# Experts 1 to 7 in order of token count, loaded from addresses read at run time

## The chip, the cores and the metric

One core of a Trainium2 chip runs the whole program. The metric is the device time of one execution in microseconds (us); lower is better.

## The reference

The program is a decoder trunk of two layers on 256 tokens of width 1024, in float32. Each layer is a mixer (a convolution group and a gated group) and a feed-forward part. The first layer's feed-forward part is dense; the second's, which the change is about, routes every token to the best two of eight experts:

```python
def moe_swiglu(h, router, wg, wu, wd):
    ht = h.reshape(B * S, D)                       # 256 x 1024
    logits = jnp.einsum('td,de->te', ht, router)   # 256 x 8
    top_vals, top_idx = lax.top_k(logits, TOP_K)   # TOP_K = 2
    gates = jax.nn.softmax(top_vals, axis=-1)
    dense_gate = jnp.sum(jax.nn.one_hot(top_idx, 8) * gates[..., None], axis=1)
    out = jnp.zeros_like(ht)
    for e in range(8):                             # wg, wu: 1024 x 2816, wd: 2816 x 1024
        out = out + dense_gate[:, e:e + 1] * swiglu(ht, wg[e], wu[e], wd[e])
    return out

def swiglu(h, wg, wu, wd):
    return (silu(h @ wg) * (h @ wu)) @ wd
```

The 256 tokens make 512 token slots, 64 for an expert on average; how many each expert gets depends on the input.

## The kernel before

Mixer 0, the dense part and mixer 1 come first, and their instructions are ordered by a small planner in the kernel. The experts' stage, `moe`, is written out in program order.

**Weights.** The host lays all weights out as blocks of 128 x 2048 floats (1 MiB each) in the order in which they are used. An expert has 33 of them: 8 for hidden chunk 0, 8 for chunk 1, 6 for chunk 2, and 4, 4 and 3 for the rows of the down projection that belong to these chunks. A load (`load_raw`, line 306) is one DMA of one block from SyncE's queue. There is a ring of 19 buffers (`rawof`, tile name `wraw`); `upto` issues loads ahead as far as the ring goes, so SyncE waits until the load 19 places earlier has had its last use, and then issues. The addresses are constants. The first 19 expert loads are all of expert 0 and are issued during mixer 1, before the routing is known.

**Slots.** An expert's tokens get slots in groups of 32, and at most three groups (`NG = 3`, 96 slots). `one_hot` makes a 0/1 matrix of tokens by slots; `gather` multiplies it with the normalised tokens to get the slots' columns `xg`, for two experts at a time: experts 0 and 1 ahead of the stage, and the pairs after that in the middle of experts 1, 3 and 5.

**Products.** TensorE (PE) holds the slots of one group (32 columns, repeated on four column strips) and streams the weights past them (`side_by_side`, line 1249), so that a group costs the same whatever number of tokens it holds. `hidden` is one chunk of gate and up products (`pg`, `pu`, for chunk 2 also `pgu`), `turn` transposes the chunk (`ptr`), `down` multiplies it by its rows of the down projection (`mpd`), `back` (`ppt`) turns the one-hot matrix, and `combine` (`pcomb`) puts the results back in token order and adds them to the residual `xs` with the gate as a factor. On PE an expert's order is: chunk 0, the last part of the down projection of the expert before and its combine, chunk 1, down 0, chunk 2, `back`, (gather), down 1.

**The third group.** It runs only if the expert has more than 64 tokens. For every one of the six stages of an expert (`hidden` three times, `down` three times) `arms` does groups 0 and 1 and then branches on the count, which PE has read into a register:

```python
def arms(c, body, blank):
    body(range(NG - 1))
    with tc.If(c > (NG - 1) * GW) as full:
        body((NG - 1,))
    with full.Else():
        blank()
```

`blank` (line 1255) is a product with zeros that opens and closes the third group's PSUM region. The branch itself stands at line 1235. Transposes, `back` and `combine` do three groups for every expert.

**More than 96 tokens.** At the end all engines read the largest count and skip a further pass (`further`) when it fits 96 slots.

Of the kernel before, what the change touches and what calls it, by code (L numbers as in the profile page):

```python
# [33 lines left out]

NG = 3
# [133 lines left out]
def weight_plan():  # L169
# [48 lines left out]
    def expert_loads(key, w, e, c0, n, k0, k1):  # L218
        per = 2048 // n
        plan[key, e] = plan.get((key, e), [])  # L220
        for k in range(k0, k1, per):
            plan[key, e].append(len(loads))
            loads.append([(w, (0, e), k, k + per, c0, n)])

    def rows(e, b):
        expert_loads(f"d{b}", "moe_wd", e, 0, D, 8 * b, min(8 * b + 8, KF))

    for e in range(E):
        for b in range(3):
            for c0, n in (WIDE[b:b + 1] if b < 2 else WIDE[b:]):  # L230
                for w in ("moe_wg", "moe_wu"):
                    expert_loads(f"h{b}", w, e, c0, n, 0, KD)
            if b or e:
                rows(e - (b == 0), (b - 1) % 3)
    rows(E - 1, 2)
    return loads, units, plan, rest


def weight_blocks(inputs):

    import numpy as np
    loads = weight_plan()[0]
# [12 lines left out]
def hybrid_trunk(  # L255
# [28 lines left out]
    st = dict(next=0, load=0, split=0, ahead=0)  # L284
# [14 lines left out]
    def load_raw(i, h=None):  # L299
        n = sum((k1 - k0) * w for _, _, k0, k1, _, w in loads[i])  # L300
# [93 lines left out]
    def upto(i):  # L394

        for j in range(st["ahead"], min(i + 1, len(loads))):
# [33 lines left out]
    G.memset(tri8, 1.0)  # L430
    G.affine_select(out=tri8, in_=tri8, compare_op=OP.is_gt, fill=0.0, base=0,
                    pattern=[[1, E], [-1, E]], channel_multiplier=0)
# [83 lines left out]
    def mixer(l, sg, nxt, rt=None):  # L516
        with ExitStack() as c2:
# [514 lines left out]
            def e_slots(t):  # L1032
# [14 lines left out]
                small(lambda: rt.one_hot(rt.oh, 0, t), (("pos", t),), (("oh", t),), 0.335)  # L1047
                if t:
                    small(lambda: V.tensor_copy(rt.icnt, pp[:, 2 * E:3 * E]), (nm,), ("icnt",), 0.075)
# [111 lines left out]
    class Route:  # L1161


        def __init__(self, pool, top):
# [11 lines left out]
            self.icnt = pool.tile([P, E], I32, name="icnt")  # L1176
# [8 lines left out]
        def one_hot(self, oh, e0, t):  # L1185
            V.tensor_tensor(oh[:, t], iot[:, None, :SL].to_broadcast([P, 2, SL]),
                            self.pos[:, t, e0:e0 + 2, None].to_broadcast([P, 2, SL]), op=OP.is_equal)

    def moe(sg, rt):
        with ExitStack() as c2:  # L1190
            gup = c2.enter_context(tc.tile_pool(name="gu", bufs=4, space=PSUM))
            pdp = c2.enter_context(tc.tile_pool(name="pd", bufs=2, space=PSUM))
            r, xn, pos, gate = sg.r, rt.xn, rt.pos, rt.gate
            st["late"] = c2.enter_context(tc.tile_pool(name="late", bufs=LATE_RAW, side="right"))
            pool = c2.enter_context(tc.tile_pool(name="experts", bufs=1))
            zero = pool.tile([P, 512], BF16, name="zero")
            G.memset(zero, 0.0)
# [6 lines left out]
            def next_pair(e0):  # L1204
                rt.oh = rt.one_hot_tile()
                for t in range(NT):
                    rt.one_hot(rt.oh, e0, t)

            def gather(e0):

                xg = rt.pool.tile([P, KD, 2 * SL], F32, name="xg", tag="big0") if e0 // 2 % 2 else pool.tile([P, KD, 2 * SL], F32, name="xg")
                oh = rt.oh

                def part(k2, ps, eng):
                    for q in range(2):
                        k = k2 * 2 + q
                        for t in range(NT):
                            T.matmul(ps[:, q * 2 * SL:(q + 1) * 2 * SL], xn[:, t, k * P:(k + 1) * P],
                                     oh[:, t].rearrange("p e s -> p (e s)"), start=(t == 0), stop=(t == NT - 1))
                    copy(eng, xg[:, k2 * 2:k2 * 2 + 2].rearrange("p k s -> p (k s)"), ps[:, :4 * SL])  # L1220
# [7 lines left out]

            def arms(c, body, blank):

                body(range(NG - 1))
                if c is None:
                    body((NG - 1,))
                    return
                with tc.If(c > (NG - 1) * GW) as full:
                    body((NG - 1,))
                with full.Else():
                    blank()
# [13 lines left out]
            def blank(banks, w):  # L1252

                b, o = divmod((NG - 1) * w, 512)
                T.matmul(banks[b][:, o:o + w], zero[:, :P], zero[:, :w], start=(o == 0), stop=True, skip_group_check=True)  # L1255

            def hidden(e, b, xg, c):
# [4 lines left out]
                o = e % 2 * SL  # L1262
                w = 256 if b < 2 else 128
                nb = -(-NG * w // 512)
# [7 lines left out]
                def body(gs):  # L1272
                    def x_(k):
                        return lambda g, q: xg[:, k, o + g * GW:o + (g + 1) * GW]
                    nl = 4 * w // 256
                    for j in range(2):
                        for k in range(KD):
                            side_by_side(banks[j], w, gs, x_(k), k == 0, k == KD - 1, [cols(nl * j, k, 4 * w, q * w, w) for q in range(4)])
                    if both:
                        for k in range(KD):  # L1280
                            side_by_side(both, P, gs, x_(k), k == 0, k == KD - 1, [cols(2 * nl + q // 2, k, 256, q % 2 * P, P) for q in range(4)])

                def blanks():
                    for v in banks:
                        blank(v, w)
# [286 lines left out]
```

## Time and profile before

| what | value |
|---|---|
| median of 3 runs | 1195.4 us (1195.16 to 1205.32) |
| the profiled execution: its own time | 1198.35 us |
| the profiled execution: its span, first to last instruction | 1196.6 us |
| experts' stage, first product of expert 0 to the last down part of expert 7 | 399.69 to 1172.40 us |
| what stands behind that (last down part, combine, final norm, output) | 24.2 us |
| mean granted TensorE clock | 0.961 |

The profile's time lies 1.75 us over its span. Busy times are those of one engine; TensorE's products are pipelined and their ends are modelled, so that "busy" is not "at its peak", and a product's start is the surer number.

### The profile page before, as it was taken

Reading aid. Unit: us, or ns where it says so; the run is one execution under the profiler, and the core shown is the slowest. Engines: PE = TensorE matmul, PEld = TensorE weight load, DVE = VectorE, ACT = ScalarE, POOL = GpSimd, SP = SyncE. Lnnn points to the kernel's source line nnn. Section 1 sums busy time; section 2 is a strip of 40 time slices with the busy share of each in tenths; the row PEclk is TensorE's granted clock in tenths of the full one; section 3 lists DMA queues with packets and bytes.
Section 4 is the critical chain, followed back from the end, with each engine's and each line's share of the span. In section 5 each row is a group of like instructions: output and inputs, shape, how many; then the busy total and the mean of one; then the engine's idle time right before and its main releaser. Section 6 shows DMA issues by size and latency. Waiting matters only on the chain. (4 is left out here: it accounts for less than half of the span.)

```text
span 1196.6 us, 33425 instructions
## 1 busy us (share of the span) xinstructions
PE 1072.5 (90%) x15484; PEld 791.6 (66%) x15484; DVE 319.6 (27%) x641; ACT 277.5 (23%) x474; POOL 143.9 (12%) x115
## 2 busy tenths in 40 slices
PE   8999999999999986986998997799799889989884
PEld 7767888887978645555656655556656666677562
DVE  5985555545895100010010010010001000100102
ACT  6665444444684000000000000100000010000002
POOL 3872000000895000000000000000000000000001
PEclk9999999999999887998999998999999999999998
DMA  8934455454843599999699789978969966888951
GB/s 308 392 133 150 176 178 183 176 202 141 304 147 121 223 420 369 369 377 366 280 401 409 314 342 369 374 299 349 407 243 382 378 272 236 368 360 349 391 206 39
DMA packets 52002, 344.06 MB, mean 288 GB/s; under 512 B 6596, under 2 KB 8444, under 8 KB 11388
## 3 DMA queue, kind: packets, MB, share of 16 engines
q1 hardware_dynamic: 48876, 339.40, 71.4%
q8 instruction: 143, 2.34, 0.8%
q10 hardware_dynamic: 2960, 2.13, 0.6%
q14 instruction: 23, 0.19, 0.0%
HBM read 340.46 MB, written 1.05 MB: 285 GB/s over the span
## 5 line engine op out<-in xcount | busy, mean ns | idle before, releaser
L1249 PE MATMUL mpd<-wraw,ah 128*32 128x256 f32 x3520 | 208.1, 393 | 8.3 <-issue 7.9
L1249 PE MATMUL pu<-wraw,xg 128*32 128x256 f32 (+1 forms) x3840 | 189.2, 351 | 19.4 <-issue 19.4
L1249 PE MATMUL pg<-wraw,xg 128*32 128x256 f32 (+1 forms) x3840 | 183.8, 345 | 12.4 <-DVE xs L1370 6.7
L1249 PEld LDWEIGHTS mpd<-wraw,ah 128*32 128x32 f32 x3520 | 124.3, 114 | 86.0 <-issue 22.3
L1249 PEld LDWEIGHTS pu<-wraw,xg 128*32 128x32 f32 x3840 | 124.7, 113 | 76.9 <-issue 22.3
L1249 PEld LDWEIGHTS pg<-wraw,xg 128*32 128x32 f32 x3840 | 118.2, 110 | 71.9 <-issue 10.8
L315 ACT ACTIVATE whi<-wraw 128x1024 fp32r<-128x1024 f32 x110 | 116.4, 1059 | 117.0 <-PE pd L376 31.1
L1293 DVE TENSOR_TENSOR sg<-sg,pu 128x512 f32<-128x512 f32 (+2 forms) x40 | 21.7, 554 | 447.0 <-ACT sg L1292 236.8
L1292 ACT ACTIVATE sg<-pg 128x512 f32<-128x512 f32 (+2 forms) x40 | 19.6, 490 | 473.5 <-PE pg L1255 143.8
L320 DVE TENSOR_TENSOR wlo<-wraw,whi 128x1024 fp32r<-128x1024 f32 x73 | 89.3, 1224 | 84.1 <-ACT whi L315 82.5
L1435 POOL TENSOR_TENSOR wraw<-xs,wraw 128x512 f32<-128x512 f32 (+1 forms) x4 | 3.9, 1002 | 793.1 <-DVE xs L1370 793.1
L320 POOL TENSOR_TENSOR wlo<-wraw,whi 128x1024 fp32r<-128x1024 f32 x37 | 89.2, 2430 | 14.4 <-ACT whi L315 13.5
L824 DVE SCALAR_TENSOR_TENSOR acc<-big,cwt,acc 128x256 f32<-128x256 f32 x199 | 86.8, 481 | 1.7
L1227 ACT ACTIVATE ah<-ptr 128x512 f32<-128x512 f32 (+1 forms) x24 | 13.5, 561 | 179.6 <-PE ptr L1307 179.6
L1249 PE MATMUL pgu<-wraw,xg 128*32 128x128 f32 x1280 | 44.0, 288 | 12.4 <-issue 12.4
L1249 PEld LDWEIGHTS pgu<-wraw,xg 128*32 128x32 f32 x1280 | 39.8, 117 | 14.6 <-issue 14.5
L757 PE MATMUL mm<-xh,whi 128*128 128x256 f32 x128 | 37.7, 294 | 2.0 <-ACT whi L315 2.0
L759 PE MATMUL mm<-xh,wlo 128*128 128x256 f32 x128 | 36.5, 285 | 0.5 <-DVE wlo L320 0.5
L343 PE MATMUL pu<-whi,xh 128*128 128x512 f32 (+1 forms) x96 | 36.5, 381 | 0.0
L758 PE MATMUL mm<-xl,whi 128*128 128x256 f32 x128 | 36.5, 285 | 0.0
L343 PE MATMUL pg<-whi,xh 128*128 128x512 f32 (+1 forms) x96 | 36.2, 377 | 0.0
L344 PE MATMUL pg<-wlo,xh 128*128 128x512 f32 (+1 forms) x96 | 36.1, 376 | 0.0
(226 smaller groups left out, 1253.1 us busy)
## 6 DMA issues: line engine op xcount, KB each, us to landing
wraw<-in_blocks_dram SPq DMA_DIRECT2D x316, 1024.0 KB, 11.7
wraw<-in_blocks_dram SPq DMA_DIRECT2D x10, 512.0 KB, 10.4
xs<-in_x_dram SPq DMA_DIRECT2D x2, 512.0 KB, 7.5
wst<-in_sgu_w_dram ACTq DMA_DIRECT2D x2, 256.0 KB, 15.4
grow<-in_norm_ffn_dram ACTq DMA_DIRECT2D x2, 256.0 KB, 3.2
wraw<-in_norm_final_dram SPq DMA_DIRECT2D x1, 512.0 KB
out_dram<-wraw SPq DMA_DIRECT2D x4, 128.0 KB, 2.2
out_dram<-wraw SPq DMA_DIRECT2D x2, 256.0 KB
```

The lines of the kernel that those rows point to most:

```text
L315: A.activation(ready[i][0][:, :w], src, AF.Copy)
L320: eng.tensor_sub(ready[i][1][:, :w], src, ready[i][0][:, :w].bitcast(F32))
L343: T.matmul(bank, xs_[0][:, c, sl], w, start=first, stop=False)
L344: T.matmul(bank, xs_[0][:, c, sl], lo, start=False, stop=False)
L757: T.matmul(o, hi[:, ws], xt[0][:, k], start=(k == 0), stop=False)
L758: T.matmul(o, hi[:, ws], xt[1][:, k], start=False, stop=False)
L759: T.matmul(o, lo[:, ws], xt[0][:, k], start=False, stop=(k == KD - 1))
L824: V.scalar_tensor_tensor(accp, src, wv, accp if w else pa, op0=OP.mult, op1=OP.add)
L1227: A.activation(o, i, AF.Copy)
L1249: T.matmul(region(banks, w, g, q), x_(g, q), srcs[q], start=first and g % (512 // w) == 0, stop=last, skip_group_check=True)
L1292: A.activation(h[:, i, :n], banks[0][i][:, :n], AF.Silu)
L1293: V.tensor_tensor(h[:, i, :n], h[:, i, :n], banks[1][i][:, :n], op=OP.mult)
```

## The change

Expert 0 stays first and is loaded from constant addresses. The other seven go in order of their token count, largest first. `places`, on VectorE, ranks the counts, writes the first block of each place's expert into an integer tile, and moves positions and counts from expert order to place order; the gates follow among the operations that are done beside expert 0. SyncE reads one integer for each place (`value_load`) and adds the block's number to it, so that the loads of places 1 to 7 have register addresses. The host lays out the blocks expert by expert, with the same blocks in the same order inside an expert.

The number of groups is fixed by place, `GROUPS = (3, 3, 3, 3, 3, 2, 2, 2)`, and there is no branch in the main pass: `arms`, `blank`, the zero tile and PE's reading of the counts are gone, and each stage goes over all its groups inside its loop over weight rows. Transposes, `back` and `combine` do only the groups of the place. Gathers are for place 0 alone (ahead of the stage), then for pairs 1-2, 3-4, 5-6 (in the middle of places 0, 2 and 4) and for place 7 alone (in place 6). The further pass runs if a place's count is over its slots.

```diff
+GROUPS = (3, 3, 3, 3, 3, 2, 2, 2)
 ...
     def load_raw(i, h=None):
+        if i < rest["load"]:
+            src = lambda cs: blocks[i, :, cs]
+        else:
+            e, j = loads[i]
+            if e == 0:
+                src = lambda cs: blocks[rest["load"] + j, :, cs]
+            else:
+                if e not in st["at"]:
+                    st["at"][e] = nc.sync.value_load(st["place"][0:1, e:e + 1], ...)
+                src = lambda cs: blocks[bass.ds(st["at"][e] + j, 1), :, cs].rearrange("o p c -> (o p) c")
 ...
-                nc.sync.dma_start(rawof[i][:, cs], blocks[i, :, cs])
+                nc.sync.dma_start(rawof[i][:, cs], src(cs))
 ...
+        def sorting(self, pool):
 ...
+            for e in range(E):
+                G.memset(self.cap[:, e:e + 1], float(GROUPS[e] * GW))
+                G.memset(self.e8[:, e:e + 1], float(e))
+                G.memset(self.base[:, e:e + 1], float(rest["load"] + e * LOADS))
+            earlier(self.tri)
 ...
+        def pick(self, o, v):
+            V.tensor_tensor(self.sort[0], self.order, v[:, None, :].to_broadcast([P, E, E]), op=OP.mult)
+            V.tensor_reduce(o, self.sort[0], axis=AX.X, op=OP.add)
+
+        def places(self):
+            c, (gt, eq) = self.crank, self.sort
+            V.tensor_copy(c, self.cnt)
+            V.tensor_scalar(c[:, 0:1], c[:, 0:1], 1024.0, None, op0=OP.add)
+            other, mine = c[:, None, :].to_broadcast([P, E, E]), c[:, :, None].to_broadcast([P, E, E])
+            V.tensor_tensor(eq, other, mine, op=OP.is_equal)
+            V.tensor_tensor(gt, other, mine, op=OP.is_gt)
+            V.tensor_tensor(eq, eq, self.tri, op=OP.mult)
+            V.tensor_tensor(gt, gt, eq, op=OP.add)
+            V.tensor_reduce(self.first, gt, axis=AX.X, op=OP.add)
+            V.tensor_tensor(self.order, self.first[:, None, :].to_broadcast([P, E, E]),
+                            self.e8[:, :, None].to_broadcast([P, E, E]), op=OP.is_equal)
+            self.pick(self.first, self.base)
+            V.tensor_copy(self.place, self.first)
+            for t in range(NT):
+                self.pick(self.ppos[:, t], self.pos[:, t])
+            self.pick(self.pcnt, self.cnt)
 ...
-            def arms(c, body, blank):
-            def blank(banks, w):
-            def hidden(e, b, xg, c):
+            def hidden(e, b, xg, ng):
 ...
+                for j in range(2):
+                    for k in range(KD):
+                        side_by_side(banks[j], w, range(ng), x_(k), k == 0, k == KD - 1, ...)
 ...
             xg, steps = gather(0, 1)
             for j, f in enumerate(steps):
                 f(lambda: gu_tile("pgat"), V if j % 2 else A)
+            rt.places()
 ...
             def largest():
+                V.tensor_sub(rt.pcnt, rt.pcnt, rt.cap)
 ...
+            def by_place(t):
+                rt.pick(rt.pgate[:, t], gate[:, t])
 ...
-            experts(xg, lambda e: nc.tensor.value_load(rt.icnt[0:1, e:e + 1], min_val=0, max_val=S), ...)
+            experts(xg, GROUPS, lambda e: later if e == 0 else ())
 ...
-            with tc.If(cnt > SL):
+            with tc.If(cnt > 0):
```

## Rows read from the trace of the kernel before

**Rows 1.** The page: engines' busy time, and the costliest group of products.

```profile
PE 1072.5 (90%) x15484; PEld 791.6 (66%) x15484; DVE 319.6 (27%) x641; ACT 277.5 (23%) x474; POOL 143.9 (12%) x115
...
L1249 PE MATMUL mpd<-wraw,ah 128*32 128x256 f32 x3520 | 208.1, 393 | 8.3 <-issue 7.9
```

**Rows 2.** Busy time by window, experts 0 to 7: length, engines, clock, DMA.

```profile
399.69:481.64 81.95, 66.47 (x1227) 45.39 (x1227) 6.25 (x24) 5.37 (x12) 0.00 (x0) 0.88 0.86 349
481.64:578.39 96.75, 77.92 (x1403) 54.25 (x1402) 8.52 (x20) 8.34 (x18) 0.00 (x0) 0.93 0.92 374
578.39:680.87 102.48, 95.08 (x1939) 63.81 (x1938) 7.28 (x16) 6.15 (x13) 0.00 (x0) 0.97 0.84 340
680.87:776.07 95.20, 80.74 (x1452) 54.05 (x1451) 8.52 (x20) 8.34 (x18) 0.00 (x0) 0.93 0.90 364
776.07:877.48 101.41, 91.55 (x1940) 61.80 (x1939) 7.27 (x16) 6.15 (x13) 0.00 (x0) 1.00 0.85 346
877.48:989.79 112.31, 102.52 (x2019) 70.94 (x2018) 8.61 (x20) 8.33 (x18) 0.00 (x0) 0.97 0.81 325
989.79:1089.34 99.55, 93.67 (x1987) 66.95 (x1986) 7.27 (x16) 6.14 (x13) 0.00 (x0) 1.00 0.82 331
1089.34:1172.40 83.06, 73.12 (x1420) 48.11 (x1419) 7.53 (x17) 6.60 (x15) 0.00 (x0) 0.96 0.70 278
```

**Rows 3.** Waits of PE's products from 480 us: sum, times, longest.

```profile
PE pg L1255 <- issue: 19.0, 5, 5.6
```

**Rows 4.** Waits of SyncE's queue, whole span: sum, times, longest.

```profile
SPq L306 <- PE pg L1249: 149.0, 11, 19.7
```

**Rows 5.** Two windows in which loads are queued; last columns: DMA share, GB/s.

```profile
1104.00:1124.00 20.00, 18.65 (x334) 11.60 (x326) 4.60 (x12) 1.25 (x3) 0.00 (x0) 1.00 0.99 395
1054.00:1068.00 14.00, 11.18 (x367) 10.21 (x359) 0.42 (x1) 0.60 (x1) 0.00 (x0) 1.00 1.02 420
```

**Rows 6.** PE's timeline in expert 3, two groups: zero products and the gather.

```profile
725.13 0.37 PE L1255 MATMUL pg<-zero 128*128 128x256 bf16 x1 [3.43 <-issue]
...
725.65 9.63 PE L1249 MATMUL mpd<-wraw,ah 128*32 128x256 f32 x128
...
758.26 0.29 PE L1255 MATMUL pg<-zero 128*128 128x128 bf16 x1 [5.08 <-issue]
...
758.69 2.79 PE L1348 MATMUL ppt<-ident,oh 128*32 128x128 f32 x48
...
764.82 7.11 PE L1249 MATMUL mpd<-wraw,ah 128*32 128x256 f32 x128
772.11 0.85 PE L1307 MATMUL ptr<-ident,sg 128*128 128x128 f32 x6 [0.18 <-PEq L1235]
```

**Rows 7.** PE's timeline in expert 6, three groups: start, length, what, idle before.

```profile
1003.63 3.64 PE L1249 MATMUL pg<-wraw,xg 128*32 128x256 f32 x64
...
1010.54 7.95 PE L1249 MATMUL mpd<-wraw,ah 128*32 128x256 f32 x144
...
1019.23 2.87 PE L1365 MATMUL pcomb<-eo,pt 32*128 32x256 f32 x48
1023.05 7.11 PE L1249 MATMUL pg<-wraw,xg 128*32 128x256 f32 x128 [0.95 <-DVE xs L1370]
...
1063.43 0.97 PE L1249 MATMUL pu<-wraw,xg 128*32 128x128 f32 x28 [1.95 <-issue]
...
1069.65 0.97 PE L1249 MATMUL pgu<-wraw,xg 128*32 128x128 f32 x28 [2.53 <-issue]
1070.44 0.27 PE L1249 MATMUL pg<-wraw,xg 128*32 128x128 f32 x1
...
1075.88 1.07 PE L1348 MATMUL ppt<-ident,oh 128*32 128x128 f32 x29
```

**Rows 8.** The window of the gather ahead of the stage.

```profile
392.44:399.69 7.25, 7.25 (x32) 7.03 (x32) 0.68 (x2) 0.98 (x2) 0.00 (x0) 0.74 0.93 391
```

**Rows 9.** VectorE's operations of the routing, by shape: busy, mean ns.

```profile
L1025 DVE TENSOR_TENSOR dg<-lg 128x64 f32<-128x64 f32 x2 | 1.5, 746 | 0.1
```

More of the change, by code (lines that the diff above doesn't have):

```diff
@@ L216, in weight_plan, with expert_loads, expert_blocks @@
     rest = dict(load=len(loads))
[L218 to L226, printed above, removed]
+    def expert_loads(key, e):
+        first = {"h0": 0, "h1": 8, "h2": 16, "d0": 22, "d1": 26, "d2": 30, "end": 33}
+        last = list(first.values())[list(first).index(key) + 1]
+        plan[key, e] = list(range(len(loads), len(loads) + last - first[key]))
+        loads.extend((e, j) for j in range(first[key], last))
     for e in range(E):
         for b in range(3):
-            for c0, n in (WIDE[b:b + 1] if b < 2 else WIDE[b:]):
-                for w in ("moe_wg", "moe_wu"):
-                    expert_loads(f"h{b}", w, e, c0, n, 0, KD)
+            expert_loads(f"h{b}", e)
             if b or e:
-                rows(e - (b == 0), (b - 1) % 3)
-    rows(E - 1, 2)
+                expert_loads(f"d{(b - 1) % 3}", e - (b == 0))
+    expert_loads("d2", E - 1)
     return loads, units, plan, rest
+LOADS = 33
+def expert_blocks(e):
+    out = []
+    for w, i0, i1 in (("h", 0, 1), ("h", 1, 2), ("h", 2, 4), ("d", 0, KF)):
+        if w == "d":
+            out += [("moe_wd", (0, e), k, k + 2, 0, D) for k in range(0, KF, 2)]
+        else:
+            out += [(m, (0, e), k, k + 2048 // n, c0, n) for c0, n in WIDE[i0:i1] for m in ("moe_wg", "moe_wu") for k in range(0, KD, 2048 // n)]
+    assert len(out) == LOADS
+    return [[v] for v in out]
 def weight_blocks(inputs):
     import numpy as np
-    loads = weight_plan()[0]
+    loads, _, _, rest = weight_plan()
+    loads = loads[:rest["load"]] + [v for e in range(E) for v in expert_blocks(e)]
     out = np.zeros((len(loads), P, 2048), np.float32)
@@ L282, in hybrid_trunk @@
     loads, units, plan, rest = weight_plan()
-    st = dict(next=0, load=0, split=0, ahead=0)
+    st = dict(next=0, load=0, split=0, ahead=0, at={})
     ready, rawof, slot = {}, {}, {}
@@ L1175, in __init__ @@
             self.cnt = pool.tile([P, E], F32, name="cnt")
-            self.icnt = pool.tile([P, E], I32, name="icnt")
+        def sorting(self, pool):
+            self.sort = [pool.tile([P, E, E], F32, name=f"sort{i}") for i in range(2)]
+            self.order = pool.tile([P, E, E], F32, name="order")
+            for nm in ("crank", "pcnt", "first", "cap", "e8", "base"):
+                setattr(self, nm, pool.tile([P, E], F32, name=nm))
+            self.ppos, self.pgate = (pool.tile([P, NT, E], F32, name=nm) for nm in ("ppos", "pgate"))
+            self.place = pool.tile([P, E], I32, name="place")
+            self.tri = pool.tile([P, E, E], F32, name="tri")
+            st["place"] = self.place
+            for e in range(E):
[3 more added lines that the diff above has]
+            earlier(self.tri)
         def x_tile(self, nm, i):
@@ L1324, in turn, with down @@
                 return x_
-            def down(e, b, x_, pd, c):
+            def down(e, b, x_, pd, ng):
                 ids = plan[f"d{b}", e]
@@ L1361, in combine @@
                 for t in range(NT):
-                    for g in range(NG):
+                    for g in range(ng):
                         for q in range(4):
@@ L1369, in combine, with experts @@
                     for t in range(NT):
[L1370 removed]
+                        V.scalar_tensor_tensor(xs[:, t, cs], ps[q][:, t * 256:(t + 1) * 256], rt.pgate[:, t, e:e + 1], xs[:, t, cs],
                                                op0=OP.mult, op1=OP.add)
[L1373 removed]
+            def experts(xg, groups, beside):
                 pend = None
                 def close():
[L1378 to L1380 removed]
+                    e, x_, pd, pt, ng = pend
+                    down(e, 2, x_, pd, ng)
+                    return combine(e, pd, pt, ng)
                 for e in range(E):
[L1383 to L1384 removed]
+                    ng = groups[e]
+                    h = hidden(e, 0, xg, ng)
                     steps = None
```

181 lines of the change are left out of this document (82 added, 99 removed).

## Prediction

> **What bounds the kernel now.** I read the page first: PE is busy 90% of the span and no other engine over 27% [rows 1]. That is a mean over stages, so I cut the experts' stage into its eight experts [rows 2]. Seven of them take 81.95 to 102.48 us and expert 5 takes 112.31, 772.7 us together of a span of 1196.6. The counts of PE products in the second column sort them: experts 2, 4, 5 and 6 have 1939 to 2019 products, the others 1227 to 1452. So four experts have over 64 tokens, and expert 0 is not one of them. The page says the same in one number: a group needs 22 row blocks x 4 column quarters = 88 down products, each of two instructions (with one, 3520 would be 40 groups, and eight experts have 24 at most); 3520 / 176 = 20 groups = 8 x 2 + 4 [rows 1]. It also says that no further pass ran, which would have added 24, so no expert has over 96.
>
> Then the two lists of waits. PE's waits from 480 us on are headed by the zero products, 19.0 us of "issue" in five pieces up to 5.6 us [rows 3]; no load stands in that list. SyncE's list is the other way round: the loads wait for PE to free buffers, 149.0 us for `pg` alone [rows 4]. So the stage goes at PE's pace, loads are ahead of it, and SyncE has time to spare. But not much is spare in the DMA: its share is 0.70 to 0.92 [rows 2], and where loads are queued it moves 395 to 420 GB/s [rows 5], which is 2.65 to 2.50 us for a block of 1.0486 MB, 82 to 87 us for an expert's 33. An expert of three groups takes PE longer than that, one of two groups need not.
>
> Two-group experts are far from two thirds of a three-group one. The timeline of expert 3 shows why [rows 6]: the zero products behind the taken branch come 3.43 and 5.08 us late for nothing that the profile shows, and behind the first of these gaps 128 products take 9.63 us where they take 7.11 later in the same expert, the clock having fallen to the lower of its two levels. The clock's means say it too: 0.88 to 0.96 in the two-group experts, 0.97 to 1.00 in the others [rows 2]. I put these gaps down to instructions that are not there yet after a jump.
>
> **The price of a place without branches.** A three-group expert falls through its branches, so it is already a run of straight code. Expert 6 takes 99.55, with the down part of a three-group neighbour in it and no gather. Brought to the same terms: experts 2 and 4 have a two-group neighbour's down part, 48 products short of 144 in 7.95 us [rows 7], so +2.6 gives 105.1 and 104.0. Expert 5 has a gather; in expert 3 it holds up PE from 761.5 (`back` ends) to 764.8 and from 773.0 (`turn` ends) to 776.1 [rows 2, 6], 6.5 us, so expert 5 is 105.8. The mean is 103.6. It has gaps in it in plain code, where nothing branches: 1.95 and 2.53 us in expert 6 [rows 7]. Without those 4.5 expert 6 is 95.0, so the mean place has 8.6 us of gaps; I keep them at that, as the mean of four.
>
> What a third group costs [rows 7]: chunk 0 and chunk 1 from 1003.63 to 1010.54, 6.9 each; down 0 and 1, 64 products of 55 ns, 3.5 each; down 2, 2.6; chunk 2 from 1070.44 to 1075.88, 5.4. That is 28.8 us, 26.2 without down 2.
>
> **The sum by places.** Place 0 is expert 0, now of three groups: 103.6 less 7.9 (no down part before it), less 3.8 (no combine, 1019.23 to 1023.05 [rows 7]), plus the gather for places 1-2, 6.5: 98.4. Places 1 and 3: 103.6 each. Places 2 and 4 with a gather: 110.1 each. Place 5: 103.6 - 26.2 - 1.1 (a third of `back`, which is some 2.2 us, and of the transposes) - 2.9 (a third of the gaps, since they come with the number of instructions) = 73.4. Place 6: 73.4 - 2.6 - 1.0 (a third of the combine's 2.87) + 5 for a gather of one place = 74.8; no row has that gather, it lies between half of 6.5 and 6.5. Place 7: 73.4 - 3.6 = 69.8. Together 743.8 where it was 772.7: -28.9. Ahead of the stage the gather has half the columns, 7.25 us [rows 8] going to something between 3.6 and 7.25; I take 5.5, since weights are still loaded 32 times: -1.7. The last combine: -1.0. Sum -31.6.
>
> The same the other way round: by these prices the two-group experts should have taken 62.8, 78.4, 81.0 and 74.5 (their `back`, transposes and combine were of three groups, 2.1 more), and took 19.2, 18.4, 14.2 and 8.6 more [rows 2], 60 us in all. The change buys back these 60 with one group more (21 for 20, since place 0 does three and needs two): 28.8 and its gaps 2.9.
>
> **What is added off the path.** `places` is 17 VectorE operations behind the gather's copies. The nearest row is 746 ns for a first 128x64 operation [rows 9], so 3 to 13 us; VectorE has nothing to do for PE until chunk 0 ends, some 20 us later, and the stage leaves it over 85% idle [rows 2]. If they took longer, PE would wait at the first transposes. The six more beside expert 0 (gates, largest) stand ahead of chunk 1's product on VectorE and have 20 us as well. GpSimd's 26 small fills are ahead of that, with GpSimd idle through the stage [rows 2]. The first dynamic load is number 30, and SyncE reaches it when load 11 is free, in the middle of chunk 1, over 20 us after `places`: its seven register reads wait for nothing, and what is queued behind them is loads that have buffers' worth of lead. PE's reading of counts goes; products run beside it already, so nothing. Address arithmetic on SyncE has no row: from nothing, since SyncE waits 149 us for one kind of product alone [rows 4], up to the 2.5 us of a load itself, at which it would begin to set the pace. I take nothing.
>
> **The loads at the end.** Sorting puts the short places last. When place 5 starts, 162 loads are used up and at most 19 more issued; 83 remain for 73.4 + 74.8 + 69.8 + 5.4 = 223 us of PE. At 2.50 us that is 208 us, at 2.65 it is 220: just hidden. What stalls vanish in these places cannot all be gained.
>
> **A rule against the trace.** Plain code shows gaps of 2 us and more at the narrow products of chunk 2 [rows 7]. The Trainium skill, "Runtime: NRT & Kernel Launch", section "Instruction fetch mechanics", says that a jump out of the fetched blocks stalls, but also that crossing a 16 KiB block in straight code is mostly hidden. By the second half the gaps of plain code would vanish; the trace does not agree here, and I hold to its gaps. The time by that rule is a rival below.
>
> **Rivals.**
> 1. Fewer gaps: buffers are now freed one by one inside a stage and not after the branch, so loads come evenly, and the gaps may be those of expert 6 (4.5) throughout. That is 4.1 less in five places and 2.7 in three: 1135. If they go altogether, 60 us less, with the loads of the end (208 us) just not in the way: 1104. Against it: three of four experts have 9 us and more.
> 2. The loads bound the tail: at 2.9 us a load at a dynamic address, 83 take 241, 18 over PE: 1182. For it: the thin margin. Against it: the loads are of the same size on the same queue.
> 3. Slower: the gaps do not belong to the jumps but to fetching beside a full DMA queue, and stay where the places are short. Then three two-group places keep the mean of 15 each: +45, 1209. It decides from 10.5 us per place. For it: gaps in plain code exist, and sorted short places run with the DMA full. Against it: a fall-through branch costs nothing, and the longest gaps stand at the zero products. Dynamic loads of 3.1 us and more end there as well, since 103.6 / 33 = 3.14 is what a long place allows.
> 4. It doesn't do what it says: a place overflows and the further pass adds eight experts, some 800 us. The counts exclude it: four experts over 64, none of them expert 0, and four such places.
>
> **How the numbers follow.** The profiled execution has 1198.35 us, 1.75 over its span; -31.6 gives 1166.8. It ran 3 us over the median, so for the median 1195.4 - 31.6 = 1164. Chances: the forecast 0.66 (own range 1148 to 1180, gaps from 6.5 to 10.5 a place), rival 1 0.17, rival 2 0.07, rival 3 0.09, rival 4 0.01. A range of 1140 to 1184 leaves out half of rival 1, half of rival 2 and rivals 3 and 4. A measurement here tells about 1% from no change: faster than 1183.4 has 0.86, within 1% 0.07, slower 0.07.
>
> **What would show it.** Right: no product at the zero tile; PE instructions for 21 groups (mpd x3696); places 1 to 4 at 100 to 111 us, 5 to 7 at 66 to 77; no wait of PE for a load; clock near 1.00 throughout. Wrong: places 5 to 7 over 80 us, with waits for loads (rival 2) or for issue (rival 3); long places far under 100 (rival 1); a load's time to landing grown; PE late at the first transposes because of `places`.

## The result and the profile after

The changed kernel takes 1146.24 us (median of 4 runs, 1143.75 to 1153.23), the kernel before beside it 1198.29 (4 runs, 1195.16 to 1205.32): a ratio of 0.9567, 95% interval [0.9503, 0.9632]. The forecast was 1164, in a range of 1140 to 1184. The profiled execution has 1143.75 us and a span of 1142.0, where before had 1196.6: 54.6 less, for which the forecast had 31.6.

The page of the changed kernel: busy times, the bandwidth in 40 slices of the span, the instruction queue (transfers, MB, share), the down products, and the loads (their median time from issue to landing last).

```profile
PE 1065.1 (93%) x15994; PEld 790.3 (69%) x15994; DVE 316.5 (28%) x650; ACT 273.7 (24%) x469; POOL 144.5 (13%) x140
GB/s 299 421 90 178 190 175 187 179 178 203 208 253 138 139 417 404 260 345 339 373 322 363 389 275 313 340 385 305 380 344 327 323 420 418 418 418 419 418 410 80
...
q8 instruction: 127, 2.08, 0.7%
...
L1301 PE MATMUL mpd<-wraw,ah 128*32 128x256 f32 x3696 | 205.7, 379 | 1.3 <-issue 1.0
...
wraw<-in_blocks_dram SPq DMA_DIRECT2D x316, 1024.0 KB, 7.1
```

There are 176 more down products than in [rows 1], one group, and PE is busy 7.4 us less all the same. The idle time before the down products is 1.3 us where it was 8.3.

Busy time by window in the changed kernel, places 0 to 7 and what follows them (columns as in [rows 2]):

```profile
398.19:493.00 94.81, 88.92 (x1828) 61.16 (x1827) 11.46 (x50) 7.18 (x16) 0.00 (x0) 1.00 0.92 364
493.00:590.65 97.65, 93.36 (x1988) 66.97 (x1987) 7.10 (x16) 6.05 (x13) 0.00 (x0) 1.00 0.89 338
590.65:697.62 106.97, 100.86 (x2019) 69.84 (x2018) 8.43 (x20) 8.12 (x18) 0.00 (x0) 0.98 0.88 344
697.62:797.55 99.93, 94.11 (x1987) 63.05 (x1986) 7.10 (x16) 6.04 (x13) 0.00 (x0) 1.00 0.88 336
797.55:901.00 103.45, 99.19 (x2020) 68.31 (x2019) 8.43 (x20) 8.13 (x18) 0.00 (x0) 1.00 0.92 349
901.00:974.28 73.28, 67.88 (x1389) 46.00 (x1388) 5.45 (x12) 4.89 (x10) 0.00 (x0) 0.98 0.97 398
974.28:1049.09 74.81, 68.60 (x1357) 47.26 (x1357) 6.02 (x15) 6.36 (x15) 0.00 (x0) 0.98 1.01 418
1049.09:1119.02 69.93, 63.32 (x1326) 43.52 (x1325) 5.02 (x11) 5.08 (x11) 0.00 (x0) 1.00 0.97 398
1119.02:1142.00 22.98, 7.39 (x128) 4.55 (x128) 6.83 (x19) 5.53 (x16) 4.90 (x6) 0.75 0.15 51
```

The eight places come to 720.8 us (forecast 743.8, before 772.7 [rows 2]). The clock is 0.98 to 1.00 in every place, where the two-group experts had 0.88 to 0.96. The stage starts 1.5 us earlier, and what stands behind it is 1.2 us shorter. So the 54.6 are 1.5 + 51.9 + 1.2. The 1.5 say little: in the runs below, with all but the same code ahead of it, the stage starts at 396.8 to 403.1 us.

PE's waits from 380 us on (us in all, times, longest), and SyncE's over the same stretch:

```profile
PE pu L1301 <- issue: 17.9, 11, 2.8
PE pgu L1301 <- issue: 11.6, 5, 2.9
PE pg L1301 <- DVE xs L1412: 6.6, 7, 1.0
```

```profile
SPq L329 <- PE pg L1301: 167.0, 65, 7.1
SPq L329 <- PE mpd L1301: 137.8, 63, 7.3
SPq L329 <- PE pu L1301: 130.8, 60, 5.0
```

Nothing heads PE's list now that belongs to a jump: the pieces of "issue" stand at `pu` and `pgu`, which are the 128-column products of chunk 2. No load is among PE's waits. SyncE waited for `pg` 11 times, 19.7 us at the longest [rows 4]; now it is 65 times and 7.1. Buffers come free one by one, and a load lands 7.1 us after its issue in the median, where the page of before has 11.7.

PE's timeline in chunk 2 of place 7 (start, length, what, idle before):

```profile
1093.41 3.70 PE L1301 MATMUL pg<-wraw,xg 128*32 128x128 f32 x128
1096.93 2.78 PE L1301 MATMUL pu<-wraw,xg 128*32 128x128 f32 x91
1101.22 1.18 PE L1301 MATMUL pu<-wraw,xg 128*32 128x128 f32 x35 [1.51 <-issue]
1102.14 0.34 PE L1301 MATMUL pgu<-wraw,xg 128*32 128x128 f32 x2
1102.23 0.28 PE L1301 MATMUL pu<-wraw,xg 128*32 128x128 f32 x2
1102.24 2.67 PE L1301 MATMUL pgu<-wraw,xg 128*32 128x128 f32 x89
1107.82 1.18 PE L1301 MATMUL pgu<-wraw,xg 128*32 128x128 f32 x35 [2.90 <-issue]
```

From one gap to the next there are 35 + 2 + 2 + 89 = 128 products. The page's instruction queue brought 2.08 MB in 127 transfers, 16.4 KB each; over PE's 15994 products that is 130 bytes for a product with its weight load, so a transfer holds some 126 of them, if the queue is PE's (products and weight loads are 31988 of the 34945 instructions of the span). The gaps stand one transfer apart. PE runs through 128 of them in 3.5 us at 27 ns, and the two gaps end 6.6 us apart, in a place whose DMA moves 398 GB/s in the mean.

The trace also holds the transfers of this queue one by one, though no view prints them. In this stretch they start at 1092.84, 1098.86 and 1105.32 us. The last two end at 1099.93 and 1106.39, and PE goes on at 1101.22 and 1107.82, 1.3 and 1.4 us later. So it is over the whole stage: the 16 pauses of 0.8 us and more between PE's instructions at the gate and up products of chunk 2, two in each place, all end 1.3 to 1.6 us after a transfer of this queue has ended. A transfer takes some 1.1 us.

### The profile page after: what moved, and what is told of

The parts are those of the page before. It is cut to its first block, busy times and chain, and to the rows that moved or that the text cites. A ratio compares the mean times of both kernels' runs of the same rounds, so it can differ in the third digit from the quotient of the medians.

```text
span 1142.0 us, 34945 instructions
## 1 busy us (share of the span) xinstructions
PE 1065.1 (93%) x15994; PEld 790.3 (69%) x15994; DVE 316.5 (28%) x650; ACT 273.7 (24%) x469; POOL 144.5 (13%) x140
## 3 DMA queue, kind: packets, MB, share of 16 engines
q8 instruction: 127, 2.08, 0.7%
## 4 chain that ended last, share of the span: by engine, by line
PE 87%; DVE 4%; issue 4%; ACT 2%; DMA 2%; POOL 1%; DVEq 0%; ACTq 0%; POOLq 0%
PE mpd L1301 18%; PE pg L1301 16%; PE pu L1301 16%; PE pd L399 5%; PE mm L982 4%; PE pgu L1301 4%; PE ptr L1281 2%; PE pg L367 2%; PE pu L366 2%; PE pg L366 2%; PE pu L367 2%; PE pu L368 2%; PE pg L368 2%; PE pcomb L1407 2%; DVE acc L850 2%
## 5 line engine op out<-in xcount | busy, mean ns | idle before, releaser
L1301 PE MATMUL mpd<-wraw,ah 128*32 128x256 f32 x3696 | 205.7, 379 | 1.3 <-issue 1.0
L1301 PE MATMUL pg<-wraw,xg 128*32 128x256 f32 (+1 forms) x4032 | 187.1, 344 | 8.0 <-DVE xs L1412 6.6
L1301 PEld LDWEIGHTS pg<-wraw,xg 128*32 128x32 f32 x4032 | 122.0, 110 | 68.9 <-DVE xs L1412 10.2
L1332 DVE TENSOR_TENSOR sg<-sg,pu 128x512 f32<-128x512 f32 (+2 forms) x34 | 18.4, 565 | 388.4 <-PE pu L1301 388.4
L1290 ACT ACTIVATE ah<-ptr 128x512 f32<-128x512 f32 (+2 forms) x24 | 13.2, 548 | 233.8 <-PE ptr L1348 150.2
L1331 ACT ACTIVATE sg<-pg 128x512 f32<-128x512 f32 (+2 forms) x34 | 15.9, 498 | 197.0 <-PE pg L1301 170.8
L1301 PE MATMUL pgu<-wraw,xg 128*32 128x128 f32 x1344 | 45.0, 290 | 11.7 <-issue 11.6
L1301 PEld LDWEIGHTS pgu<-wraw,xg 128*32 128x32 f32 x1344 | 41.5, 117 | 13.6 <-issue 13.6
L1354 DVE TENSOR_TENSOR ah<-ah,ptr 128x192 f32<-128x192 f32 (+1 forms) x8 | 2.6, 329 | 124.0 <-ACT ah L1353 124.0
```

Source lines behind the costliest of these rows:

```text
L1301: T.matmul(region(banks, w, g, q), x_(g, q), srcs[q], start=first and g % (512 // w) == 0, stop=last, skip_group_check=True)
```

## The experiments

All are made from the changed kernel. Lengths of places are read as in the windows above; "gaps" are what a place takes over its length without loads (the fourth experiment), which is PE's idle time and what its products lose at a lower clock. In the diffs `...` stands for lines that are not shown.

**1. The old order of the groups, without a branch.** `hidden` and `down` go over all weight rows with groups 0 and 1, then again with group 2:

```diff
-                for j in range(2):
-                    for k in range(KD):
-                        side_by_side(banks[j], w, range(ng), x_(k), ...)
+                for gs in (range(min(2, ng)), range(2, ng)):
+                    for j in range(2):
+                        for k in range(KD):
+                            side_by_side(banks[j], w, gs, x_(k), ...)
 ...
```

> The changed kernel, but each stage does groups 0 and 1 over all its weight rows and then group 2 over all of them again, in straight code: same products, no branch, buffers freed only behind group 2 as in the kernel before. Theory A (long places got shorter than forecast because buffers are freed one by one, so loads are thin beside chunk 2 and instructions come sooner): places 0 to 4 go back from 94.8, 97.7, 107.0, 99.9, 103.5 us to about 98, 104, 110, 104, 110, +23 us, about 1169. Theory B (straight code alone did it): places stay within 1 us, 1146 give or take 5. Places 5 to 7 are untouched in both.

It took 1161.78 us, ratio 0.9695 [0.9646, 0.9744]. Places 0 to 4 took 99.6, 103.6, 106.6, 101.6 and 108.4, 17.0 us over those above; places 5 to 7, which have no third group, stayed (73.2, 74.1, 70.3). Two windows from each kernel show how: the first 13.5 us of chunk 2 in places 1 and 4. First the changed kernel, then this one:

```profile
558.28:571.78 13.50, 10.44 (x368) 9.97 (x368) 0.42 (x1) 1.02 (x2) 0.00 (x0) 1.00 0.96 365
862.83:876.33 13.50, 11.06 (x387) 10.52 (x390) 0.42 (x1) 1.03 (x2) 0.00 (x0) 1.00 0.96 351
```

```profile
564.97:578.47 13.50, 10.45 (x367) 9.91 (x367) 0.43 (x1) 0.54 (x1) 0.00 (x0) 1.00 1.01 418
876.76:890.26 13.50, 10.00 (x344) 9.49 (x347) 0.43 (x1) 0.54 (x1) 0.00 (x0) 1.00 1.02 420
```

In this order a block is free only when group 2 has read it, so the blocks of chunk 1 come free together, and their loads run at 418 to 420 GB/s through the chunk whose products are narrowest. In these 13.5 us PE gets as far in place 1 (368 and 367 products) and not in place 4 (387 and 344); over chunk 2 and `back` of the five long places this order takes 14.5 us more, most of the 17.0. SyncE's waits say the same:

```profile
SPq L329 <- PE pg L1301: 296.3, 57, 19.3
```

The longest wait is 19.3 us again, as before [rows 4].

**2. The branch back in places 5 to 7.** The old branch and zero products, for these places alone:

```diff
-GROUPS = (3, 3, 3, 3, 3, 2, 2, 2)
+GROUPS = (3, 3, 3, 3, 3, 3, 3, 3)
...
+            def arms(e, ng, body, blank):
+                if not 5 <= e:
+                    body(range(ng))
+                    return
+                body(range(NG - 1))
+                c = counts(e)
+                with tc.If(c > (NG - 1) * GW) as full:
+                    body((NG - 1,))
+                with full.Else():
+                    blank()
...
```

> The changed kernel, but places 5 to 7 have the old branch back: groups 0 and 1, a branch on the count, which skips group 2 for these three, and zero products; transposes, back and combine do three groups there. Theory A (a taken jump costs instructions that are not there yet): each of the three goes up by the 15 us that a two-group expert lost before and 2 for the third share of back, transposes and combine, +51 us, about 1197. Theory B (the gaps come with the amount of code and loads, not with jumps): +6 us, about 1152.

It took 1200.61 us, ratio 1.0045 [1.0021, 1.0069]: all that the change had gained is gone. The three places:

```profile
903.28:992.25 88.97, 72.90 (x1419) 48.92 (x1419) 7.27 (x16) 6.27 (x13) 0.00 (x0) 0.96 0.79 317
992.25:1089.64 97.39, 78.34 (x1403) 54.49 (x1402) 8.40 (x20) 7.87 (x18) 0.00 (x0) 0.89 0.97 388
```

The third took 83.06. Together they are 269.4 against 218.0, 51.4 us for three branching places.

**3. The same branches without loads**, to part the jump from the loads beside it. The two edits of experiments 2 and 4 together.

> The old branch in places 5 to 7, and the 231 loads of places 1 to 7 left out (the output is not the reference's). With loads the branch cost 51.4 us over the fixed groups in these three places (269.4 against 218.0). Theory A, what follows a jump comes late whatever the DMA does: places 5 to 7 take 198.5 + 51 = 250 us, the run 1150. Theory B, a jump costs only because its instructions are fetched beside full loads: 198.5 and some 6 for transposes, back and combine of a third group, 205; the run 1105. Between them, some 225, both count.

It took 1135.41 us, ratio 0.9473 [0.9421, 0.9524], and the three places 75.9, 81.1 and 75.1: 232.2 where straight code without loads takes 198.5:

```profile
880.26:956.16 75.90, 70.62 (x1420) 47.09 (x1419) 7.27 (x16) 6.26 (x13) 0.00 (x0) 0.98 0.01 4
956.16:1037.29 81.13, 74.05 (x1404) 51.14 (x1403) 8.25 (x20) 7.85 (x18) 0.00 (x0) 0.94 0.01 3
1037.29:1112.42 75.13, 68.90 (x1372) 49.40 (x1371) 7.17 (x16) 6.48 (x14) 0.00 (x0) 0.95 0.04 10
```

So 33.7 of the 51.4 stay. Some 6 of them are for the transposes, `back` and combine of a third group (an estimate, 2.1 a place by the prediction's prices). That leaves some 28 us that come with the jumps alone, and some 18 come only beside loads. Of the 28, 14.7 are PE's waits for "issue" and for its sequencer; the rest is mostly products at a lower clock, 0.94 to 0.98 where straight code without loads has 1.00. Neither theory holds by itself. PE's timeline in chunk 2 of place 5 shows both, first in experiment 2, then here:

```profile
970.30 5.15 PE L1306 MATMUL pgu<-wraw,xg 128*32 128x128 f32 x119 [2.52 <-issue]
980.79 0.29 PE L1329 MATMUL pg<-zero 128*128 128x128 bf16 x1 [5.35 <-issue]
```

```profile
937.80 3.68 PE L1314 MATMUL pgu<-wraw,xg 128*32 128x128 f32 x128
944.68 0.23 PE L1337 MATMUL pg<-zero 128*128 128x128 bf16 x1 [3.20 <-issue]
```

The zero product behind the jump is 3.20 us late with nothing on the DMA, and 5.35 beside loads; the gap ahead of `pgu`, in plain code, is gone without loads. The transfer of instructions that ends the wait at the zero product starts 3.2 us after the last PE instruction before the jump beside loads, and 1.2 us after it without; either takes some 1 us.

**4. No loads beside the products.** The 231 loads behind the first 33 are left out, which are all but three of those of places 1 to 7 and three of place 0, and the products read the block that lies 19 loads back in the ring:

```diff
     def place(i):
+        if again(i):
+            rawof[i], slot[i] = rawof[i - 19], slot[i - 19]
+            return
...
+    def again(i):
+        return i >= rest["load"] + LOADS
+
     def load_raw(i, h=None):
+        if again(i):
+            return
```

> The changed kernel, but only the first 33 expert blocks are loaded; later places multiply what lies in the ring (231 loads left out). Theory A (gaps in straight code come from fetching instructions beside loads): the gaps of the last seven places vanish, places 1 to 4 near 94, 101, 94, 101 us and 5 to 7 near 68, 70, 64, about 30 us less, 1115. Theory B (narrow products outrun the fetch whatever the loads do): places as before within 2 us, 1146.

It took 1098.82 us, ratio 0.9176 [0.9127, 0.9226], and the places 89.28, 93.93, 100.34, 94.45, 100.34, 66.56, 68.25 and 63.69: 676.8 us.

```profile
sum 676.82, PE 665.51 PEld 462.32 DVE 58.95 ACT 51.82 POOL 0.00; mean PE 83.19 PEld 57.79 DVE 7.37 ACT 6.48 POOL 0.00
```

All of "issue" is gone from PE's list but one piece of 0.2 us. The gaps of the changed kernel are therefore 720.8 - 676.8 = 44 us, more than the 30 that I expected. Chunk 2 with `back` holds nearly all of them. By the sums of windows from its first product to the last one of `back`, in all eight places, first of the changed kernel, then without loads:

```profile
sum 161.98, PE 129.39 PEld 123.73 DVE 6.16 ACT 12.21 POOL 0.00; mean PE 16.17 PEld 15.47 DVE 0.77 ACT 1.53 POOL 0.00
```

```profile
sum 119.64, PE 119.40 PEld 118.93 DVE 6.16 ACT 12.17 POOL 0.00; mean PE 14.93 PEld 14.87 DVE 0.77 ACT 1.52 POOL 0.00
```

42.3 of the 44 are in there: 32.4 of idle time of PE and 10.0 of products that take longer, the granted clock being 0.90 to 0.93 in three of the eight windows and 1.00 in all of them without loads. In place 7 the transfers of instructions now start 3.5 us apart, where they were 6.0 and 6.5, and take 0.93 to 0.98 us where they took 1.07: they hardly get shorter, they start in time. What the fourth experiment alone leaves open is whether it is the loads' traffic, or PE's waits for them.

**5. The old order of the groups without loads.** Edits 1 and 4 together.

> Groups 0 and 1 over all weight rows and then group 2, and the 231 loads of places 1 to 7 left out (their products read blocks of expert 0 again, so the output is not the reference's). With loads this order cost 16.9 us in the long places. Theory A, the order costs only through the loads that it bunches, beside which instructions come late: the eight places come to 677 us, as in the changed order without loads, and the run to 1099. Theory B, the order costs by itself (twice as many passes over the weights, other instruction addresses): places 692 to 694, the run 1114 to 1116.

It took 1098.16 us and its places 676.2: theory A. The order of the groups costs nothing by itself; its 17 us come through the loads that it bunches.

**6. Fewer loads.** Those of 8 of the 19 buffers are left out, as in experiment 4 but with

```diff
+        j = (i - rest["load"]) % (RAW_BUFS + MORE_RAW + LATE_RAW)
+        return i >= rest["load"] + LOADS and not MORE_RAW <= j < MORE_RAW + RAW_BUFS
```

> 42% of the loads of places 1 to 7 left out (those of 8 of the 19 buffers, whose old blocks are read again, so the output is not the reference's). All loads cost the eight places 44 us of gaps (720.8 against 676.8). Theory A, an instruction fetch is late by the packets queued at that moment, so only a standing queue costs: with 11 of 19 loads no place has one, nearly all of the 44 us go, places 677 to 685. Theory B, it costs in proportion to the bytes moved: 58% of 44 stay, places 702. Theory C, the gaps come with the waits of PE's instructions for loads and not with the DMA's load: also some 702, but at the products that read a loaded block.

It took 1124.67 us, its places 703.0. That is B's number, but not B's way of getting there. The same windows of chunk 2, places 0 to 7 (without loads they are 17.0 us in places 0, 1, 2 and 4, 17.8 in place 3, and 11.3 in places 5 to 7):

```profile
453.59:474.73 21.14, 19.03 (x625) 18.77 (x624) 0.98 (x2) 1.60 (x4) 0.00 (x0) 0.92 0.29 105
558.08:575.04 16.96, 16.96 (x624) 16.96 (x627) 0.98 (x2) 1.61 (x4) 0.00 (x0) 1.00 0.16 63
651.68:674.39 22.71, 19.31 (x624) 18.59 (x624) 0.98 (x2) 1.65 (x4) 0.00 (x0) 0.92 0.72 258
757.73:780.46 22.73, 19.31 (x625) 18.51 (x627) 0.98 (x2) 1.65 (x4) 0.00 (x0) 0.92 0.70 256
857.85:874.82 16.97, 16.97 (x625) 16.97 (x624) 0.98 (x2) 1.62 (x4) 0.00 (x0) 1.00 0.20 69
940.49:956.84 16.35, 11.90 (x418) 11.36 (x421) 0.42 (x1) 1.36 (x3) 0.00 (x0) 1.00 0.77 318
1008.85:1025.99 17.14, 13.51 (x416) 12.94 (x416) 0.42 (x1) 1.36 (x3) 0.00 (x0) 0.90 1.02 423
1082.97:1094.26 11.29, 11.29 (x416) 11.29 (x419) 0.42 (x1) 1.36 (x3) 0.00 (x0) 1.00 0.16 51
```

It is all or nothing. Where the DMA's share in the chunk is 0.16 to 0.20 there is no gap at all; from 0.70 on there are 4.9 to 5.9 us. The mean of 0.29 in place 0, with 4.1 us, holds a burst just ahead of its gap:

```profile
463.08:466.48 3.40, 3.40 (x129) 3.33 (x122) 0.56 (x1) 0.00 (x0) 0.00 (x0) 1.00 0.93 352
```

The transfers of instructions there start at 459.68 and 466.48 us, and the products stop until 468.78. My expectation failed in its premise: loads left out did not keep a queue from standing in some of the chunks. Theory C falls by the blocks: counted round the ring of 19, the six blocks of chunk 2 are all left out in place 5, which has its gaps, and all loaded in place 7, which has none.

**7. Addresses known ahead.** Every place loads the expert of its own number from constant addresses:

```diff
...
-                    st["at"][e] = nc.sync.value_load(st["place"][0:1, e:e + 1], ...)
-                src = lambda cs: blocks[bass.ds(st["at"][e] + j, 1), :, cs].rearrange("o p c -> (o p) c")
+            src = lambda cs: blocks[rest["load"] + e * LOADS + j, :, cs]
```

> The changed kernel, but every place loads the blocks of the expert with its own number, at constant addresses, so that places 1 to 7 multiply with other experts' weights. Theory A (register addresses cost nothing, SyncE has time to spare): 1146 give or take 6, places 5 to 7 as before within 1 us. Theory B (register addresses delay loads in the last three places, where the DMA is at 418 GB/s): 5 to 15 us less, in these three places.

1146.40 us, ratio 0.9565 [0.9522, 0.9608]: 0.16 us from the changed kernel, whose own four runs lie 9.5 apart. Places 5 to 7 took 73.4, 74.6 and 70.3. Register addresses cost nothing here.

**8. Three groups everywhere**, `GROUPS = (3, 3, 3, 3, 3, 3, 3, 3)`.

> The changed kernel with three groups in every place: straight code, sorted, three groups more. Theory A (a group costs 26 to 29 us of PE and its share of gaps): places 5 to 7 become like places 1 to 4, 98 to 107 us where they were 73.3, 74.8 and 69.9: +85 us, about 1231, with the DMA no longer at 418 GB/s at the end. Theory B (the last places are already held up by loads): less than +60, below 1206.

1232.23 us, ratio 1.029 [1.0236, 1.0343]; places 5 to 7 took 99.1, 105.9 and 94.0, 81.0 us more than with two groups, 27.0 a group. The fixed numbers of groups are worth this, and without them the change would have been a loss.

**9. The short places early**, `GROUPS = (3, 2, 2, 2, 3, 3, 3, 3)`, with the ranking turned round:

```diff
-            V.tensor_scalar(c[:, 0:1], c[:, 0:1], 1024.0, None, op0=OP.add)
+            V.tensor_scalar(c[:, 0:1], c[:, 0:1], -1024.0, None, op0=OP.add)
...
-            V.tensor_tensor(gt, other, mine, op=OP.is_gt)
+            V.tensor_tensor(gt, other, mine, op=OP.is_lt)
```

> The changed kernel in the other order: expert 0, then smallest counts first, GROUPS (3, 2, 2, 2, 3, 3, 3, 3), the same 21 groups. Theory A (the DMA's lead decides where short places may stand): behind place 0 the ring is full just as behind place 4, so that the three short places have the same 83 us of loads against 73 of PE each and a lead of 19 loads: they take 70 to 76 us as before, and the whole is within 8 us of 1146. Theory B (long places first build up a lead that the short ones at the end live on): short places in front wait for loads, 80 us or more each, 1160 to 1175.

1148.27 us, ratio 0.9598 [0.9556, 0.9639]; the short places took 73.8, 77.7 and 70.3. Sorting serves to know where the short ones are; that they come last is neither gain nor loss.

**10. Two groups in place 0**, `GROUPS = (2, 3, 3, 3, 3, 2, 2, 2)`, which is what the counts of this input ask for; another input could need the further pass.

> The changed kernel with GROUPS (2, 3, 3, 3, 3, 2, 2, 2): place 0 does the two groups that expert 0 needs on this input; the further pass still stands behind it for inputs where it needs more. Theory A (PE sets the pace up to place 0 too): place 0 falls by 26 us for the group's products without down 2, and down 2 by 2.6 in place 1, about 4 more for the smaller back, transposes, combine and gaps: 1146 - 32 = 1114. Theory B (the loads set the pace of the whole stage, since the last 200 us are at 418 GB/s): the gain of place 0 is lost in waits for loads in the last three places, 1135 or more.

1123.83 us, ratio 0.9369 [0.9312, 0.9426]. That is 22.4 us less than the changed kernel, where I expected 32. Place 0 took 70.13, 24.7 less, and the eight places 24.2 less. Neither theory has the number: no load is among PE's waits, and places 5 to 7 stayed (73.7, 74.3, 69.2), but chunk 2 of place 1 took 25.49 us where it took 21.00. The stage of the profiled execution also starts 3.3 us later, at 401.52.

**11. Wider products in chunk 2.** The host lays gate and up columns of the chunk's first 512 side by side, and PE reads them as products of 256 columns in place of two of 128:

```diff
+                if both:
+                    gu = [banks[0][0], banks[1][0]]
+                    for k in range(KD):
+                        side_by_side(gu, 256, range(ng), x_(k), k == 0, k == KD - 1, [raws[k // 2][:, k % 2 * D + q * 256:][:, :256] for q in range(4)])
-                for j in range(2):
+                for j in range(0 if both else 2):
...
```

> The changed kernel with the first two thirds of chunk 2 read as products of 256 columns (gate and up columns side by side in the blocks) in place of two runs of 128 columns: 384 products for 576 in a place of three groups, the same columns and bytes. All but 2 of the 44 us of gaps lie in chunk 2. Theory A, TensorE there uses up a 16 KiB piece of instructions every 3.6 us, which is faster than one arrives beside full loads (6.2 us): at half the instructions per column only the last third of chunk 2 outruns them, some 2 us of gap stay of 5.5 in each place, the places come to about 693 us and the run to 1118 to 1122. Theory B, the gaps belong to this stage whatever its number of instructions (its buffers, its reading of SBUF beside the loads): no change, 1146. Less than A if the loads take over in places 5 to 7, whose last loads land 8 us ahead of their use: then 1122 to 1126.

1128.79 us, ratio 0.9405 [0.9357, 0.9452]: 17.5 us less than the changed kernel. The eight windows of chunk 2 come to 137.7 where they were 162.0, as theory A says; theory B falls. But the places came to 707.3, not 693, since the last one took 77.1. PE's timeline there, and PE's waits from 380 us on:

```profile
1063.19 1.93 PE L1306 MATMUL pu<-wraw,xg 128*32 128x256 f32 x32 [0.38 <-DMA wraw<-in_blocks_dram]
1065.69 1.93 PE L1306 MATMUL pu<-wraw,xg 128*32 128x256 f32 x32 [0.56 <-DMA wraw<-in_blocks_dram]
1068.27 1.93 PE L1306 MATMUL mpd<-wraw,ah 128*32 128x256 f32 x32 [0.65 <-DMA wraw<-in_blocks_dram]
```

```profile
PE mpd L1306 <- DMA wraw<-in_blocks_dram: 5.8, 5, 2.1
PE pgu L1306 <- issue: 4.5, 3, 2.3
PE pgu L1306 <- DMA wraw<-in_blocks_dram: 2.6, 2, 2.1
```

A block's 32 products take 1.9 us, and start every 2.5 us: the loads now set the pace at the end, 10.9 us of waits for blocks in all, with the `pg` and `pu` ones, some 8.9 of them in this place. The loads bounding the tail is the prediction's rival 2, come true one step later, at 2.5 us a load and not its 2.9.

**12. Both together**, the wide chunk 2 and two groups in place 0.

> The same chunk 2, and two groups in place 0 as the counts of this input allow (they are not known ahead, so this is a bound for this input and not a kernel for any). With narrow products two groups in place 0 gave 1123.8. Theory A: 25 us less than that less what the loads take back, since place 0 is now short as well and the DMA full in it: 1097 to 1105. Theory B: 1124.

1094.88 us, ratio 0.9137 [0.909, 0.9184]: 51.4 us under the changed kernel, 28.9 under experiment 10, and the fastest that was run. The stage is 671.4 us; its last place is held by the loads as in experiment 11 (77.9 us, at 415 GB/s).

## Why the prediction was right, and what it missed

**Direction and mechanism.** The two-group places were to take 73.4, 74.8 and 69.8 and took 73.28, 74.81 and 69.93. That they agree to 0.2 us is in part luck: without loads the three take 198.5 us where the forecast had 200.9, and their gaps are 19.5 where it had 17.1. Experiment 2 puts the branch back and they cost 51.4 us more; so the gaps of the old two-group experts belong to the branch, some 18 of the 51 through the loads beside it (experiment 3), and rival 3 falls. What it said of fetching beside a full queue is there, at 6.5 us a short place, under the 10.5 from which it would have decided. The fixed group in place 0 costs less than was said of it: 24.2 us over the eight places of experiment 10 (22.4 by the medians) and 27.0 a group in experiment 8 (28.7 by the medians), against 28.8 and 2.9 of gaps.

**The term that was mis-sized** is the gap in a long place: "the mean place has 8.6 us of gaps; I keep them at that". Places 0 to 4 were to take 525.8 us and took 502.8. Without loads they take 478.3, so their gaps are 24.5 us, 4.9 a place, where the forecast had 43. The other 4.5 of the 23 are the straight code itself, forecast at 482.8. Experiment 1 shows why 8.6 was no price for the new code: in the old order, without any branch, the same five places take 519.8, which is 41.5 of gaps, 8.3 a place. The 8.6 was a true reading of the kernel before, and it belonged to the order in which its buffers come free. The diff moves the group loop inside the loop over weight rows; I had that down under rival 1, at a chance of 0.17, and charged the forecast nothing for it. Rival 1 took it to be worth 4.1 a long place and 2.7 a short one, 1135 in all. It is worth 3.7 in the long ones and nothing in the short ones, whose gaps are 6.5 (19.5 in three) against my 5.7: with no third group there is no order to change, and the DMA's share there is 0.97 to 1.01. So the time lies between the forecast and rival 1. Gaps of 5.5 us a place in the mean are outside the 6.5 to 10.5 that the forecast gave itself, and 1146.24 is outside its own 1148 to 1180; the stated 1140 to 1184 holds it because it took in half of rival 1. Places 1 and 3, at 97.65 and 99.93 us, also lie under the 100 to 111 that were to show it right.

**The small terms.** The gather went from 7.25 to 5.75 us (forecast 5.5); the same 32 products took 7.0 in experiment 10, at a granted clock of 0.51 where it was 0.63, so this term is known to some 1 us only. The end is 1.2 us shorter (1.0). The 17 operations of `places` ran from 398.57 to 402.4 on VectorE, 3.8 us of the 3 to 13 allowed, and PE waited for none of them. The loads at register addresses cost nothing (experiment 7), as assumed.

**The loads of the end.** They were "just hidden", and were: at 398 to 418 GB/s in places 5 to 7, with no wait of PE. How thin the cover is shows experiment 11.

**The rule set against the trace.** In plain code the trace of after shows gaps still, 44 us of them, so the time of 1104 at which they vanish was rightly kept for a rival. The Trainium skill, "Runtime: NRT & Kernel Launch", section "Instruction fetch mechanics", calls a crossing in straight code mostly hidden and a taken branch out of the fetched blocks a stall. The runs here agree with the first where the DMA is idle (576 narrow products to a long place, and 0.2 us of "issue" in all of experiment 4), not beside a standing queue of loads; with the second they agree in both cases (3.20 and 5.35 us).

**What stays open.** That instructions come late beside loads is shown by the gaps that appear and vanish with the traffic in chunk 2, and by the transfers themselves: they take some 1.1 us with loads and without, and start late beside them. What they wait for before they start is not seen in the trace, and holding back the loads during chunk 2 alone was not tried.

## What to carry to other kernels

Take the price of a stall from code with the same order of work: a gap read from the old kernel carries the old order of buffer releases in it. Where a branch skips a known share of the work, sorting by size and fixing the sizes by place can buy back the jumps, here 17 us a place of 70. When loads fill the queue, look first at the stage with the narrowest products, and once that is faster, at the loads of the last stage.

## What the runs showed of the hardware

- PE's straight code starves beside loads when its products are short: at 128 columns it uses a transfer of instructions in 3.5 us, and in experiment 6 chunks at a DMA share of 0.70 or more lost 4.9 to 5.9 us, those at 0.20 or less nothing; the gate and up products of 256 columns (7 us a transfer) waited for no instructions in experiment 11.
- The transfer of instructions is hardly slower beside loads, it starts later: in place 7 of the changed kernel they start 6.0 and 6.5 us apart and take 1.07 us, without loads 3.5 us apart and 0.93 to 0.98. After each of the 16 pauses of chunk 2, PE goes on 1.3 to 1.6 us after one has ended.
- A jump in PE's stream costs without any load beside it: some 28 us in three places of six branches each, about half of it waits and the rest mostly a lower clock behind them.
- Loads at addresses from a register are as fast as those at constant ones: 1146.24 against 1146.40 us for 231 of them.
